# State-space units every 14.4 attention steps in place of 15, and four idle sub-steps in place of eight ahead of the gate products

## The chip, the cores and the metric

One core of one Trainium2 chip runs the whole program. The metric is the device time of one execution in microseconds (us), the median of several executions. The engines are PE (TensorE: matrix products and transposes), DVE (VectorE), ACT (ScalarE), POOL (GpSimd) and SP (SyncE, which here only issues transfers). A transfer is issued by an engine's queue, takes that queue some tenths of a us, and lands later.

## The reference, cut to what matters

One layer of a streaming encoder: 2048 frames of width 1024. A normalised input is projected once; a quarter of the columns, `u`, goes to a state-space mixer, the rest are queries, keys and values of chunked attention. Both results are normalised, joined and sent through `w_out`; then a gated feed-forward network follows.

```python
bu = einsum('bsgh,gph->bsgp', u, b_bar)          # 32 groups of 16 channels, 64 complex states each
_, states = associative_scan(combine, (a, bu))   # along the 2048 frames
y = einsum('bsgp,ghp->bsgh', states, c_mat).real + d_skip * u
y = gelu(y)
y = y * sigmoid(y @ w_glu + b_glu)               # the gate products of the mixing
scores = q k^T / 8 + bias[clip(rel)]             # each 64-frame chunk sees itself and 8 before it
out = softmax(scores) v
```

## The kernel before, in words

Every matrix product is made of three passes of split operands (a high and a low part, tiles named `..h`/`..l` or `hi`/`lo`), so PE has much to do. The program goes through stages one after another: the projection of `u` (0 to 144 us), the attention loop (144 to about 738 us), the mixing (to about 1000 us), the gate and up products of the feed-forward network, and its down product (to the end). Only the attention loop and the first part of the mixing are touched by the change.

**The attention loop** (`att_phase`, L947) has 128 steps: 4 blocks of 512 frames, 8 heads, 4 query tiles. A step s does, in this order: the score products of step s (tiles `sc`, the softmax after them on DVE L846 and ACT L849), on some steps the head's output products (tiles `pj<-pth,v`), the transposes of the probabilities of step s−2 (tiles `pt`, L77; ACT L864 copies them into `pth`, DVE L865 writes the low part `ptl`), and then "filler": pieces of other work, called units. All products on PE are pinned in the order in which the program writes them, so PE never passes a product that waits.

**Units.** A unit is a Python generator with n sub-steps that is to run between attention steps s0 and s1. `Unit.advance` (L667 ff.) is called once in each step and runs as many sub-steps as a proportional rule wants by then (L672). There are units that normalise the input of the next block (`hT_unit`), that project queries and keys (`qk_unit`, tiles `pf`; DVE L775 writes the keys `k` that the scores read) and values (`v_unit`), 8 state-space units, and the mixing's beginning.

**A state-space unit** (`ssm_unit`, L560) handles 4 of the 32 groups in 42 sub-steps:

1. loads on SP (L567): `U` (8 transfers), `Bst`, `Tm` (8), `Vm`; then YL = 8 idle sub-steps;
2. two sub-steps with 4 products each, `pj<-U,Bst`, copied by ACT (L591) into X: called the **X products** here;
3. 21 sub-steps of scan on POOL (L605 to L617), which works only from X;
4. a transfer of the scanned states, `XG<-X`, 4 pieces issued by POOL (L639), then YX = 9 idle sub-steps;
5. two sub-steps with 8 products each, `pj<-U,Tm` and `pj<-XG,Vm`: the **Y products**. ACT copies the result (L649), and SP writes it out in 8 transfers (L652, `y<-X`).

U, Tm, Vm, X and XG are single buffers. The loads of the next unit's U and Tm wait until the Y products of this unit are done, and they stand behind this unit's 8 writes of y on SP. The units follow one another without a break: unit b runs from step 2 + int(SW·b) to step 2 + int(SW·(b+1)).

**The mixing's beginning** (`mix_phase`) is a unit too, of MIX_N sub-steps. At step 119 it loads the gate weights (L997 ff.). From step 122 on it loads the state-space output `yr<-y` (L1030, 4 transfers that need all of y), applies Gelu on ACT (L1034; this loads another activation table first), splits the result into `gh` and `gl` (L165, L166), waits PY idle sub-steps, and then makes the **gate products** `pf<-gh,wgh` etc. in 16 sub-steps, one of them with the norm's sums (`pf<-ones,sq`). Then it loads the second block and waits PZ sub-steps. Its last part runs after the loop.

The lines that the change's numbers enter:

```python
units.append(Unit(ssm_unit(...), SSM_N, 2 + int(SW * b), 2 + int(SW * (b + 1)), light=SL))   # L945
units += [Unit(islice(mix, MIX_N), MIX_N, GSTART, N + LAG, GSTART - OPEN)]                   # L951
want += math.ceil((self.n - 1) * self.room(self.s0, s + 1) / self.room(self.s0, self.s1) - 1e-9)
```

Of the kernel before, what the change touches and what calls it, by code (L numbers as in the profile page):

```python
# [45 lines left out]
LPH = 2  # L46
V0 = 0, 4
DB, XB = 3, 2
SW = 15
CUT = -8, -2, 2, 7, 13, 19, 24  # L50
CUTL = -8, -2, 2, 7, 13, 19, 23
ORDER = "sptf"
# [628 lines left out]
def att_phase(k, ident, S):  # L681
    tc, nc, io = k.tc, k.nc, k.io
    with ExitStack() as cx:
# [260 lines left out]
        for b in range(NG // GB):  # L944
            units.append(Unit(ssm_unit(k, sp, psum, S, b, k.ssm_eng), SSM_N, 2 + int(SW * b), 2 + int(SW * (b + 1)), light=SL))  # L945
        N = len(steps)
# [19 lines left out]
        return mix  # L966


PY, PZ = 8, 1
MIX_N = 17 + PY + PZ  # L970


# [732 lines left out]
```

## Time and profile before

| what | value |
|---|---|
| time, median of 3 executions | 2330.36 us (2327.14 to 2331.63) |
| the profiled execution's own time | 2327.38 us |
| span of the profiled execution (first to last instruction) | 2325.6 us |
| mean granted TensorE clock | 0.971 |
| attention loop, start of step 0 to start of step 127 | 144.1 to 737.8 us |
| transfers issued in the span | 437.00 MB, mean 188 GB/s |

A row of the timeline gives the start and the duration in us, the engine, the line, the operation, what it writes and reads, and in brackets for how long the engine stood idle before it and what ended that. "x8" joins eight like instructions. SPq is SP's queue of transfers. A row of the table by windows gives, for a stretch from A to B, its length, then busy time and (count) of PE, PE's weight loads, DVE, ACT and POOL, then the granted clock of TensorE (1.00 is full), the mean busy share of the transfer engines, and GB/s.

### The profile page before, as it was taken

How to read it: one execution, taken by the hardware profiler on the slowest of the kernel's cores; microseconds unless marked ns; L12 is line 12 of the kernel's file. 1: busy time of each engine (PE TensorE's matmuls, PEld its weight loads, DVE VectorE, ACT ScalarE, POOL GpSimd, SP SyncE). 2: the span in 40 equal slices, each digit the busy share in tenths (PEclk: the TensorE clock that was granted, in tenths of full speed). 3: DMA queues.
4: the chain of work that ended last, by engine and by line, in shares of the span. 5: the costliest groups of instructions: out<-in, count | busy, mean ns of one | idle time of the engine just before them, and what ended most of it. 6: DMA issues, size and time to landing. Idle time of an engine off the chain costs nothing.

```text
span 2325.6 us, 30451 instructions
## 1 busy us (share of the span) xinstructions
PE 2191.2 (94%) x10568; PEld 1839.8 (79%) x10568; DVE 1481.0 (64%) x2251; ACT 1000.5 (43%) x1675; POOL 1130.8 (49%) x1280
## 2 busy tenths in 40 slices
PE   8978899999997899989999998999999989999996
PEld 6667688898986788768888887788888778888886
DVE  7845555656556846666775667766645375578676
ACT  6335555555557542343333335333333343345322
POOL 3406645455660433565555558545555364445442
PEclk9989999999998999999999999999999999999998
DMA  8787766766643535644554556555433287465552
GB/s 296 256 280 259 226 206 199 213 194 193 187 139 114 177 122 170 227 160 149 167 192 162 195 195 239 195 194 167 156 95 110 87 321 251 163 219 181 202 186 73
DMA packets 214066, 437.00 MB, mean 188 GB/s; under 512 B 27096, under 2 KB 57864, under 8 KB 206808
## 3 DMA queue, kind: packets, MB, share of 16 engines
q1 hardware_dynamic: 209048, 420.89, 54.5%
q0 software_dynamic: 4864, 14.17, 1.9%
q8 instruction: 83, 1.36, 0.2%
q14 instruction: 71, 0.58, 0.1%
HBM read 294.98 MB, written 132.15 MB: 184 GB/s over the span
## 4 chain that ended last, share of the span: by engine, by line
PE 50%; DVE 3%; DMA 1%; issue 1%; POOL 1%; ACT 1%; SPq 0%; DVEq 0%; ACTq 0%; POOLq 0%
PE X L74 19%; PE ps L74 16%; PE Y L74 10%; PE W L74 5%; DVE sa L1554 1%; DVE lo L166 1%; DMA hd<-wc 1%; POOL c L166 0%; DMA acc<-x 0%; DVE S L1373 0%; DVE g L1438 0%; DMA hd<-hq 0%; DMA lo<-hc 0%; DVE acc L1571 0%; DVE u L1395 0%
## 5 line engine op out<-in xcount | busy, mean ns | idle before, releaser
L74 PE MATMUL X<-hi,c 128*128 128x512 f32 x1408 | 451.2, 391 | 9.1 <-ACT c L165 5.0
L74 PE MATMUL ps<-hd,hd 128*128 128x512 f32 (+1 forms) x1968 | 433.9, 382 | 7.7 <-POOL hd L166 5.4
L74 PEld LDWEIGHTS ps<-hd,hd 128*128 128x128 f32 x1968 | 359.9, 190 | 80.4 <-POOL hd L166 6.2
L166 POOL TENSOR_TENSOR c<-S,c 128x512 fp32r<-128x512 f32 x176 | 251.4, 1430 | 245.6 <-ACT c L165 244.6
L74 PEld LDWEIGHTS X<-hi,c 128*128 128x128 f32 x1408 | 265.4, 189 | 66.7 <-ACT c L165 5.4
L166 POOL TENSOR_TENSOR hd<-hd 128x1536 fp32r<-128x1536 f32 (+1 forms) x53 | 190.2, 3597 | 207.0 <-ACT hd L165 188.0
L74 PE MATMUL X<-lo,c 128*128 128x512 f32 x704 | 274.9, 390 | 0.0
L166 POOL TENSOR_TENSOR c<-raw,c 128x512 fp32r<-128x512 f32 x132 | 188.1, 1425 | 128.1 <-ACT c L165 100.6
L165 ACT CAST hd<-hd 128x1536 fp32r<-128x1536 f32 (+1 forms) x106 | 147.3, 1392 | 225.4 <-DMA hd<-hq 143.6
L74 PE MATMUL Y<-hi,c 128*128 128x512 f32 x704 | 227.2, 393 | 10.9 <-DVE u L1395 10.9
L1519 DVE TENSOR_TENSOR acc<-acc,ps 128x512 f32<-128x512 f32 x196 | 128.6, 681 | 80.8 <-PE ps L74 80.3
L74 PE MATMUL big<-m,woh 128*128 128x512 f32 x512 | 164.7, 402 | 1.9 <-DVE m L166 1.6
L74 PEld LDWEIGHTS Y<-hi,c 128*128 128x128 f32 x704 | 133.7, 190 | 40.5 <-DVE u L1395 12.6
L74 PE MATMUL pf<-hi,w 128*128 128x512 f32 x416 | 151.7, 417 | 7.3 <-ACT w L165 3.6
L165 ACT CAST c<-S 128x512 fp32r<-128x512 f32 x176 | 109.3, 622 | 111.9 <-PE Y L74 55.9
L605 POOL TENSOR_TENSOR st<-X,a 128x128 f32<-128x128 f32 (+2 forms) x136 | 47.0, 346 | 226.5 <-ACT X L591 164.8
L74 PEld LDWEIGHTS X<-lo,c 128*128 128x128 f32 x704 | 132.8, 189 | 27.4
L846 DVE CUSTOM_DVE_ANT_0 s<-sc,nb 128x640 f32<-128x640 f32 (+4 forms) x128 | 94.4, 738 | 93.3 <-PE sc L74 89.4
L1391 ACT COPY u<-X 128x512 f32<-128x512 f32 x132 | 77.1, 585 | 178.2 <-PE X L74 178.2
L165 ACT CAST c<-raw 128x512 fp32r<-128x512 f32 x132 | 82.1, 622 | 151.0 <-PE Y L74 81.3
L166 DVE TENSOR_TENSOR hd<-hd 128x1536 fp32r<-128x1536 f32 (+1 forms) x53 | 115.3, 2176 | 38.7 <-ACT hd L165 37.6
L74 PE MATMUL Y<-lo,c 128*128 128x512 f32 x352 | 138.2, 393 | 0.0
(463 smaller groups left out, 4693.5 us busy)
## 6 DMA issues: line engine op xcount, KB each, us to landing
w<-wss SPq DMA_DIRECT2D x36, 1024.0 KB, 5.7
hq<-g SPq DMA_DIRECT2D x140, 256.0 KB, 2.0
hd<-hq SPq DMA_DIRECT2D x42, 768.0 KB, 4.5
hd<-wc SPq DMA_DIRECT2D x42, 768.0 KB, 6.1
raw<-in_w_gate SPq DMA_DIRECT2D x44, 512.0 KB, 3.6
raw<-in_w_up SPq DMA_DIRECT2D x44, 512.0 KB, 4.2
wc<-px SPq DMA_DIRECT2D x66, 256.0 KB, 2.9
wss<-w SPq DMA_DIRECT2D x12, 1024.0 KB, 5.8
```

Of the source, the lines that this page charges most:

```text
L74: return self.tc.keep_in_program_order(self.tc.nc.tensor.matmul(*a, **b))
L165: (hi_eng or nc.scalar).copy(hi, raw)
L166: (lo_eng or nc.gpsimd).tensor_tensor(lo, raw, f32(hi), op=ALU.subtract)
L605: eng.tensor_tensor(t[:, :, :, :n], src, ar, op=ALU.mult)
L846: nc.vector.tensor_tensor_reduce(s[:, :nk].rearrange("p (a b) -> p a b", a=nch), ps[:, :nch, :half], hd.nb[:, nk - 1 :: -1].rearrange("p ( ...
L1391: nc.scalar.copy(u[:], ps[:])
L1519: V.tensor_tensor(a, a, ps[:], op=ALU.add)
L1554: (nc.gpsimd if m else nc.vector).tensor_tensor(self.sa[m][:, :n], self.sa[m][:, :n], t[:, :n], op=ALU.add)
```

## The change

```diff
-SW = 15
+SW = 14.4
...
-PY, PZ = 8, 1
+PY, PZ = 4, 1
 MIX_N = 17 + PY + PZ
```

SW sets where the state-space units stand, PY how many idle sub-steps lie between the Gelu of the first block and its gate products. MIX_N falls from 26 to 22, over the same steps 122 to 129. By the order of instructions, the units' products stand at the end of these attention steps:

| unit | 0 | 1 | 2 | 3 | 4 | 5 | 6 | 7 |
|---|---|---|---|---|---|---|---|---|
| X products, before | 4 | 19 | 34 | 49 | 64 | 79 | 94 | 109 |
| X products, changed | 4 | 18 | 32 | 47 | 61 | 76 | 90 | 104 |
| Y products, before | 16 | 31 | 46 | 61 | 76 | 91 | 106 | 121 |
| Y products, changed | 15 | 29 | 44 | 58 | 73 | 87 | 101 | 116 |

From X to Y there were 12 steps in every unit; now there are 11, except in units 2, 4 and 7, which keep 12. From Y to the next X there are 3 steps, before and now. No product is added or left out.

The first place is PE around the start of step 88. `pf_...` are query/key products of the filler of step 87, `sc_...` the scores of step 88, `pt_...` the transposes. Before:

```order
L74 MATMUL pf_6331<-lo_1174_4794,w_6089 128x512
L74 MATMUL pf_6331<-hi_1173_4793,w_6089 128x512
L74 MATMUL sc_6486<-k_1461_6216,q2h_6214 128x320
L74 MATMUL sc_6486<-k_1461_6216,q2l_6215 128x320
...
L77 MATMUL pt_6496<-ident_81,s_6372 128x128 x5
```

With the change:

```order
L74 MATMUL pf_6383<-lo_1178_4810,w_6149 128x512
L74 MATMUL pf_6383<-hi_1177_4809,w_6149 128x512
L74 MATMUL pj_6487<-U_5763,Tm_5774 128x256
L74 MATMUL pj_6487<-XG_2387,Vm_5783 128x256
...
L74 MATMUL pj_6493<-U_5763,Tm_5774 128x256
L74 MATMUL pj_6493<-XG_2387,Vm_5783 128x256
...
L74 MATMUL sc_6507<-k_1481_6276,q2h_6274 128x320
L74 MATMUL sc_6507<-k_1481_6276,q2l_6275 128x320
...
L77 MATMUL pt_6517<-ident_81,s_6406 128x128 x5
```

Unit 5's Y products, which stood at the end of step 91, now stand right in front of the scores of step 88. (The repetitions of the `pj` and `sc` rows are left out.)

The second place is PE at steps 123 and 124, where the gate products begin (`gh`, `gl` are the split Gelu output, `wgh`, `wgl` the split gate weights). Before:

```order
L77 MATMUL pt_8412<-ident_81,s_8265 128x128 x5
L74 MATMUL sc_8420<-k_1848_7995,q2h_7993 128x320
L74 MATMUL sc_8420<-k_1848_7995,q2l_7994 128x320
...
L77 MATMUL pt_8429<-ident_81,s_8306 128x128 x5
L74 MATMUL pf_8437<-gh_1929_8357,wgh_1892_8218 128x512
L74 MATMUL pf_8437<-gl_1930_8358,wgh_1892_8218 128x512
```

With the change:

```order
L77 MATMUL pt_8412<-ident_81,s_8286 128x128 x5
L74 MATMUL pf_8420<-gh_1929_8357,wgh_1895_8239 128x512
L74 MATMUL pf_8420<-gl_1930_8358,wgh_1895_8239 128x512
...
L74 MATMUL sc_8427<-k_1864_8047,q2h_8045 128x320
L74 MATMUL sc_8427<-k_1864_8047,q2l_8046 128x320
...
L77 MATMUL pt_8436<-ident_81,s_8306 128x128 x5
```

The first gate products stand one step earlier: ahead of the scores and transposes of step 124 in place of behind them. The 16 sub-steps of gate products are spread as 2, 3, 3, 3, 3, 2 over steps 124 to 129 before, and as 2, 2, 3, 3, 2, 3, 1 over steps 123 to 129 with the change.

The third place is ACT at the table load ahead of the Gelu (`s_...` is the exponential of the softmax, L849; `pth_...` the copy of the transposes). Before:

```order
L849 ACTIVATE s_8401,sm_8249<-s_8401,mn_8402 128x640
L864 CAST pth_8334<-pt_8412 128x5x128
L849 ACTIVATE s_8425,sm_8249<-s_8425,mn_8426 128x640
L864 CAST pth_8334<-pt_8429 128x5x128
L1034 ACT_TABLE_LOAD
```

With the change:

```order
L849 ACTIVATE s_8401,sm_8270<-s_8401,mn_8402 128x640
L165 CAST wgh_1901_8251<-sg_8253 128x512
L165 CAST wgh_1904_8257<-sg_8259 128x512
L864 CAST pth_8334<-pt_8412 128x5x128
L1034 ACT_TABLE_LOAD
```

The table load now follows the copy of the transposes that belong to step 123, one exponential and one copy earlier, with two weight copies ahead of it.

## The prediction

> **What bounds the kernel now.** The page comes first, with the engines' shares. Then the attention loop alone, in the table by windows, since only the loop and its last steps are touched.
>
> ```profile
> PE 2191.2 (94%) x10568; PEld 1839.8 (79%) x10568; DVE 1481.0 (64%) x2251; ACT 1000.5 (43%) x1675; POOL 1130.8 (49%) x1280
> ```
>
> ```profile
> 144.10:737.80 593.70, 541.21 (x3193) 482.52 (x3194) 330.58 (x638) 324.69 (x672) 294.53 (x708) 0.94 0.66 200
> ```
>
> PE bounds. In the loop it is busy for 541 of 594 us at a clock of 0.94, while DVE, ACT and POOL are busy for about half. A step takes 593.7/127 = 4.67 us. The change takes no product away, so it can only move PE's waits and what they do to the clock. So the second view is the waits of PE inside the loop, the third what the clock did behind them.
>
> ```profile
> PE pt L77 <- DVE ptl L865: 11.6, 9, 2.6
> PE pj L74 <- DMA Tm<-kts: 4.1, 3, 2.4
> ...
> PE pf L74 <- ACT gh L165: 6.8, 1, 6.8
> ```
>
> ```profile
> 225.90:229.30 3.40, 3.35 (x17) 3.02 (x18) 1.08 (x2) 0.64 (x2) 0.00 (x0) 1.00 0.63 212
> 313.30:316.70 3.40, 3.40 (x12) 2.91 (x11) 0.07 (x1) 2.57 (x7) 0.00 (x0) 0.50 0.50 107
> 422.50:425.90 3.40, 3.27 (x11) 2.79 (x12) 3.34 (x7) 2.10 (x4) 0.00 (x0) 0.50 0.96 347
> 552.20:555.60 3.40, 3.40 (x9) 2.68 (x9) 3.34 (x6) 2.13 (x4) 3.35 (x5) 0.50 0.96 351
> 651.20:654.60 3.40, 3.40 (x11) 2.93 (x10) 0.54 (x1) 2.93 (x8) 0.02 (x1) 0.50 0.56 141
> ```
>
> The last four rows lie right behind the four waits of 2.4 to 2.9 us shown below: 3.4 us at half clock, so 1.7 us of work lost. **Such a wait costs its length and 1.7 us more.** The first row, behind a wait of 2.99 us, has full clock: the price is not paid every time.
>
> **The first two units become late.** Shown: the starts of steps 16 and 17, unit 0's Y products, unit 1's X products, step 30, unit 1's Y products and step 32; then POOL's last issue of unit 1's scan, and the landing times of that transfer.
>
> ```profile
> 219.16 0.22 PE L74 MATMUL sc<-k,q2h 128*128 128x128 f32 x1
> 225.95 0.67 PE L74 MATMUL pj<-XG,Vm 128*128 128x256 f32 x2 [2.99 <-DMA XG<-X]
> 228.86 0.47 PE L74 MATMUL sc<-k,q2h 128*128 128x256 f32 x1
> 239.94 1.97 PE L74 MATMUL pj<-U,Bst 128*128 128x256 f32 x8 [0.87 <-DMA Tm<-kts]
> 284.92 0.34 PE L74 MATMUL sc<-k,q2h 128*128 128x384 f32 x1
> 293.51 0.59 PE L74 MATMUL pj<-U,Tm 128*128 128x256 f32 x2
> 296.78 0.50 PE L74 MATMUL sc<-k,q2h 128*128 128x320 f32 x1
> ```
>
> ```profile
> 285.42 1.21 POOL L639 DMA_DIRECT2D XG<-X  x2 [0.30 <-POOL X L617]
> ```
>
> ```profile
> DMA to landing us min/median/max: 7.1/7.6/8.2
> ```
>
> For all eight units together the same view has:
>
> ```profile
> DMA to landing us min/median/max: 2.3/5.0/8.4
> ```
>
> Unit 0's X products stay in step 4, so its XG lands at 225.9 as before, and PE, now at the end of step 15, comes to it at about 219.6: it waits some 6.3 us in place of 2.99. From there a chain that PE doesn't hold up runs on: Y, the writes and loads on SP (PE had to wait 0.87 us for them already), X at 239.9, the scan on POOL, XG issued until 286.6 and landed 7 us later, at about 293.5. Before, PE came to that point at 293.5 too; this is no slack. So unit 1's Y products still end at about 296.8 whatever PE does, but PE has steps 30 and 31 still ahead of it: 293.51 − 284.92 = **+8.6 us**. Behind a wait of about 4 us the products run at half clock (up to +1.7), but a landing in the whole run's median of 5 us in place of 7.6 gives as much back; I leave both out and keep 6 to 10.3 as the bounds.
>
> **Unit 2's load wait goes.** Its X products, and on SP the writes of y and loads of U ahead of them:
>
> ```profile
> 312.51 3.02 PE L74 MATMUL pj<-U,Bst 128*128 128x256 f32 x8 [2.44 <-DMA Tm<-kts]
> ```
>
> ```profile
> 299.32 3.61 SPq L652 DMA_DIRECT2D y<-X  x8
> 304.58 3.41 SPq L567 DMA_DIRECT2D U<-u  x7
> ```
>
> Before, 296.78 to 312.51 = 15.7 us from Y to X, since the writes began 2.5 us after Y and a weight load stood between the two rows. With the change the writes and the loads stand one behind the other: some 0.6 (ACT's copy) + 3.6 + 3.7 (8 loads) + about 2.5 for the landing = 10.4 us by these rows, while PE has steps 30, 31 and 32, 8.6 and a mean step of 4.7, together 13 us. The wait and its half clock vanish: **−4.1** (0 if another load slips between). Unit 3's share of the row Tm<-kts, 4.1 − 2.44 − 0.87 = 0.8, goes likewise; its XG may cost 0.5: **−0.3**.
>
> **Y products fill two waits.**
>
> ```profile
> 418.72 0.41 PE L74 MATMUL sc<-k,q2h 128*128 128x320 f32 x1
> 422.63 1.33 PE L77 MATMUL pt<-ident,s 128*128 128x128 f32 x5 [2.63 <-DVE ptl L865]
> 432.56 0.59 PE L74 MATMUL pj<-U,Tm 128*128 128x256 f32 x2
> ```
>
> ```profile
> 547.85 0.31 PE L74 MATMUL sc<-k,q2h 128*128 128x320 f32 x1
> 551.06 0.42 PE L74 MATMUL sc<-k,q2h 128*128 128x320 f32 x1 [2.76 <-DVE k L775]
> ```
>
> In steps 59 and 88 PE waits for DVE. The Y products, 296.78 − 293.51 = 3.27 us of PE's work, now stand in front of step 59 (unit 3) and of step 88 (unit 5). DVE works on meanwhile, so each wait is filled, with its half clock: −2.63 − 1.7 and −2.76 − 1.7, if the Y products themselves don't wait. For unit 5 that can be checked:
>
> ```profile
> 502.61 0.50 PE L74 MATMUL sc<-k,q2h 128*128 128x320 f32 x1
> 514.45 1.89 PE L74 MATMUL pj<-U,Bst 128*128 128x256 f32 x8
> ```
>
> ```profile
> 557.36 1.21 POOL L639 DMA_DIRECT2D XG<-X  x2 [0.30 <-POOL X L617]
> ```
>
> From X to the last XG issue 558.0 − 514.45 = 43.5, to the landing 46 to 48 (3 to 5 us); PE has from step 77 (502.61) to step 88 (547.85) 45.2: some 0.5 us short. I take **−4.0** for each, with −8 to 0 as the bounds of both. Where step 59's wait is gone, unit 4's load has steps 59 to 61, 432.56 − 418.72 − 4.3 = 9.5 us for 10.4: **+1.3** with what little the other loads may lack, +0.5 more: **+1.8**.
>
> **Unit 7's load wait goes.**
>
> ```profile
> 650.15 2.81 PE L74 MATMUL pj<-U,Bst 128*128 128x256 f32 x8 [2.89 <-DMA U<-u]
> ```
>
> X moves to step 104, away from the block boundary's own loads; three mean steps give 14 us for 10.4: −2.89 − 1.7 = **−4.6** (bounds −4.6 to 0).
>
> **The mixing's beginning.**
>
> ```profile
> 698.28 0.60 PE L74 MATMUL pj<-U,Tm 128*128 128x256 f32 x2
> 701.55 0.50 PE L74 MATMUL sc<-k,q2h 128*128 128x320 f32 x1
> 708.73 0.85 PE L77 MATMUL pt<-ident,s 128*128 128x128 f32 x5 [2.15 <-DVE ptl L865]
> 712.40 1.30 PE L77 MATMUL pt<-ident,s 128*128 128x128 f32 x5 [1.75 <-DVE ptl L865]
> 720.46 0.79 PE L74 MATMUL pf<-gh,wgh 128*128 128x512 f32 x1 [6.76 <-ACT gh L165]
> ```
>
> ```profile
> 714.45 1.28 ACT L1034 ACT_TABLE_LOAD   x1
> 715.74 3.64 ACT L1034 ACTIVATE ys<-yr 128x2048 f32<-128x2048 f32 x1
> ```
>
> The gate products wait 6.76 us for ACT, which does the table load and the Gelu only behind the copy of step 124's transposes. With the change they stand behind step 123's transposes (708.73), and the Gelu one copy earlier, so the **wait remains**: ACT's 1.28 + 3.64 us still lie between those transposes and the first gate product. The transposes are 3.7 us earlier than step 124's; two weight copies (about 0.6 each) and the wait ahead of 712.40 eat part, so the products start 2 to 3 us earlier. But step 124's scores and transposes (3.7 − 1.75 + 1.3, about 2 us at full clock) now follow them. **−0.9**, with −3 to +3 as bounds: this is an order in which I can't see which wait is then last.
>
> Four idle sub-steps fewer are not work; the new ACT copies in front of other steps may uncover waits (the page's waits have nine of `ptl` alone): **+2.0**, bounds 0 and 4.
>
> **The sum** against the profiled execution's 2327.38 us (span 2325.6): 8.6 − 4.1 − 0.3 − 4.0 − 4.0 + 1.8 − 4.6 − 0.9 + 2.0 = −5.5, so 2321.9. That execution was 3.0 under the median of the three, 2330.36; against the median it is **2325 us**.
>
> **A page's rule.** The Trainium skill, "TensorE: Matmul & The Clock Gate", Part 1 (the HAM clock gate), says that the clock halves after at least one idle window of about 3.4 us, and that the windows run free. By that rule waits of 2.4 to 2.9 us would cost no clock, and four removals would bring 4 × 1.7 us less. The rows above disagree on the length (0.50 behind all four) and agree with free-running windows in one point: the same kind of wait at 225.95 left the clock at 1.00.
>
> **The rivals.**
>
> - *The fills don't hold* at steps 59 and 88, since the DVE chains there are themselves set by PE's earlier products: +8, about 2333. For it: waits on `ptl` come nine times, they are not tied to a place. Chance 0.18.
> - *Slower: the scan doesn't fit into 11 steps.* In units 3, 5 and 6 it is as in units 0 and 1: XG lands in 8 us, as unit 1's did. Unit 5 then needs 43.5 + 8 = 51.5 against 45.3, so it waits 6 us in place of 0.5; for units 3 and 6, also 11 steps long, I take 2.5 us each (between nothing and unit 5's 6). With three half clocks of 1.7 this is 5.5 + 5.0 + 5.1 = +15.6, so about 2340. It decides where landings take more than some 5 us. For it: units 0 and 1 are already bound by this chain. Against it: all units' median landing of 5.0 us. Chance 0.20.
> - *The gate wait is hidden*: y is written 5 steps earlier; if the scheduler's order lets ACT do the Gelu before PE needs it, 6.76 + 1.7 go as well: about 2317. Against it: ACT's order puts the table load behind step 123's copy. Chance 0.12.
> - *Short waits cost no clock, and the four half clocks are due to something that stays*: 4 × 1.7 = 6.8 less gain, about 2331. For it: the window at 225.90. Against it: four of five. Chance 0.08.
>
> **How the numbers follow.** Forecast 0.42, around 2325 (2319 to 2330 by its own bounds). 0.2%, 4.7 us, is about what a measurement of this kernel can tell from no change, so faster means under 2325.7 and slower over 2335.0. Two thirds of the forecast (0.28) and the hidden gate wait (0.12) are faster: 0.40. The rest of the forecast (0.14), most of the fills that don't hold (0.13) and most of the fourth rival (0.06) are the same: 0.33. The rest, 0.27, is slower. The range reaches from within the third rival, 2315, to past the second, 2341.
>
> **What would show it.** In the changed profile: a wait of about 6 us on XG near 226 and one of about 4 near 293; no wait of 2.4 on U or Tm at unit 2's X products nor of 2.9 at unit 7's; no wait for `k` in step 88 nor for `ptl` in step 59; full clock there; still 5 to 7 us of wait on `gh`, ending near 718 plus the lag. The forecast is wrong if XG is waited for in units 3, 5 or 6 by more than 1 us, or if waits of 2 to 3 us turn up at new places.

## The result, and the profile after

The changed kernel is **slower**: 2346.60 us (median of 6, 2339.45 to 2349.81) against 2329.64 us (6 runs beside them, 2327.14 to 2331.63), a ratio of 1.007 with a 95% interval of 1.0056 to 1.0084. The forecast was 2325 us, with a range from 2315 to 2341.

Two more waits of PE before the change, from 150 to 720 us (a row has the total in us, how many waits there were, and the longest):

```profile
PE sc L74 <- DVE k L775: 6.6, 3, 2.8
...
PE pf L74 <- ACT hi L729: 3.6, 2, 2.0
```

The waits of PE in the changed kernel, from 150 to 720 us and from 720 to 1000 us:

```profile
PE pj L74 <- DMA XG<-X: 11.6, 2, 6.9
PE pj L74 <- DMA Tm<-kts: 11.2, 3, 5.7
...
PE pt L77 <- DVE ptl L865: 6.6, 7, 1.8
PE pf L74 <- ACT hi L729: 5.4, 2, 3.1
PE sc L74 <- DVE k L775: 4.3, 2, 2.7
...
PE pj L74 <- DMA U<-u: 1.3, 1, 1.3
```

```profile
PE pf L74 <- ACT gh L165: 8.5, 1, 8.5
```

The waits for XG grew from 3.0 to 11.6 us, as forecast. The waits for loads at the X products grew from 7.0 us (4.1 put down to Tm, 2.9 to U) to 12.5 (11.2 and 1.3), which was not; these products read only U and Bst, so the name Tm is not to be taken at its word. The waits for `ptl` and `k` shrank, the one for `hi` grew. The rows with these waits in the timeline of PE, in the order of the units (the XG waits of units 0 and 1, then the X products of units 2, 4, 5 and 7):

```profile
222.44 1.19 PE L74 MATMUL pj<-XG,Vm 128*128 128x256 f32 x2 [4.71 <-DMA XG<-X]
290.39 1.19 PE L74 MATMUL pj<-XG,Vm 128*128 128x256 f32 x2 [6.86 <-DMA XG<-X]
307.07 1.89 PE L74 MATMUL pj<-U,Bst 128*128 128x256 f32 x8
441.49 3.75 PE L74 MATMUL pj<-U,Bst 128*128 128x256 f32 x8 [5.67 <-DMA Tm<-kts]
515.91 3.50 PE L74 MATMUL pj<-U,Bst 128*128 128x256 f32 x8 [4.49 <-DMA Tm<-kts]
645.84 1.89 PE L74 MATMUL pj<-U,Bst 128*128 128x256 f32 x8
```

Units 2 and 7 have no wait any more, as forecast. Units 4 and 5, which had none before, wait 5.67 and 4.49 us, and their eight products take 3.75 and 3.50 us in place of 1.89: the clock is halved there, as the windows show.

```profile
443.70:447.10 3.40, 3.40 (x12) 2.88 (x10) 0.75 (x2) 2.85 (x8) 0.24 (x1) 0.50 0.87 259
515.10:518.50 3.40, 2.58 (x6) 2.17 (x7) 0.00 (x0) 0.45 (x2) 0.00 (x0) 0.57 0.36 68
```

**Where the time went, stretch by stretch.** For some attention steps up to which the same units' products are done in both kernels, the table has the start of the first score product in the two profiled executions, and the lag, after minus before. At step 61, 3.3 us of Y products that stand later before are taken off. The last attention steps can't be compared so, since the changed kernel has made two sub-steps more of gate products by step 127; behind step 112 the table goes on to the mixing's first output product (`big<-m,woh`), ahead of which both have made all of them.

| up to step | before, us | after, us | lag | gained in the stretch | forecast | what lies in it |
|---|---|---|---|---|---|---|
| 15 | 217.03 | 215.02 | −2.0 | −2.0 | 0 | nothing that was changed |
| 52 | 387.68 | 390.27 | +2.6 | +4.6 | +4.2 | units 0 to 3: 8.6 − 4.1 − 0.3 |
| 61 | 430.05 | 433.13 | −0.2 | −2.8 | −4.0 | Y products in front of step 59 |
| 66 | 456.28 | 464.64 | +8.4 | **+8.6** | +1.3 | unit 4's loads |
| 81 | 519.46 | 534.20 | +14.7 | **+6.3** | +0.5 | unit 5's loads |
| 96 | 589.20 | 605.73 | +16.5 | **+1.8** | −4.0 | Y products in front of step 88 |
| 112 | 661.97 | 673.81 | +11.8 | −4.7 | −4.6 | unit 7's loads |
| output product | 763.27 | 777.65 | +14.4 | **+2.6** | −0.9 | the mixing's beginning |
| end (span) | 2325.6 | 2346.9 | +21.3 | +6.9 | 0 | nothing that was changed |

The last row is mostly not the change's: in a run below whose text differs from before only in the queue of some loads inside the loop, the stretch behind the first output product was 4.9 us longer too (lag −10.9 there, −6.0 at the end). The profiled execution of before is 2.3 us under the median of its kernel and that of after 2.2 above, which is why the medians differ by 17.0 us and the spans by 21.3. The allowance of +2.0 for newly uncovered waits has no stretch of its own.

**What holds up units 4 and 5** is on SP's queue. After unit 3's Y products, which end at 425.3 us:

```profile
425.92 0.33 SPq L747 DMA_DIRECT2D k<-ks  x1
427.53 0.46 SPq L771 DMA_DIRECT2D q2h<-q2h  x1
428.62 0.46 SPq L772 DMA_DIRECT2D q2l<-q2l  x1
429.14 5.90 SPq L652 DMA_DIRECT2D y<-X  x8
435.13 0.37 SPq L899 DMA_DIRECT2D ya_s<-ya  x1
435.55 3.72 SPq L567 DMA_DIRECT2D U<-u  x8
```

And after unit 4's Y products, which end at 500.2 us:

```profile
500.85 1.26 SPq L652 DMA_DIRECT2D y<-X  x3
505.84 0.34 SPq L747 DMA_DIRECT2D k<-ks  x1
506.31 0.47 SPq L771 DMA_DIRECT2D q2h<-q2h  x1
507.43 0.47 SPq L772 DMA_DIRECT2D q2l<-q2l  x1
507.95 2.48 SPq L652 DMA_DIRECT2D y<-X  x5
510.47 3.23 SPq L567 DMA_DIRECT2D U<-u  x7
```

The longest wait of this queue from 494 to 518 us that holds up the rows above:

```profile
SPq L747 <- PE sc L74: 3.6, 1, 3.6
```

The writes of y, and behind them the loads of the next U, stand in one queue with the key and query copies of a `qk_unit` (L747, L771, L772). The query copies wait for ACT and DVE, and the key copy waits for score products of PE itself. The last load of U is issued 14.0 and 13.5 us after the Y products, so the products can start 16 us after them; the forecast had 10.4.

### The profile page after: what moved, and what is told of

Read it like the earlier page. It is cut to its first block, busy times and chain, and to the rows that moved or that the text cites. A ratio compares the mean times of both kernels' runs of the same rounds, so it can differ in the third digit from the quotient of the medians.

```text
span 2346.9 us, 30468 instructions
## 1 busy us (share of the span) xinstructions
PE 2195.0 (94%) x10568; PEld 1842.2 (78%) x10568; DVE 1468.7 (63%) x2251; ACT 1000.5 (43%) x1675; POOL 1131.2 (48%) x1280
## 4 chain that ended last, share of the span: by engine, by line
PE 49%; DVE 4%; DMA 1%; issue 1%; POOL 1%; ACT 1%; SPq 0%; DVEq 0%; ACTq 0%; POOLq 0%
PE X L74 19%; PE ps L74 16%; PE Y L74 10%; PE W L74 5%; DVE sa L1554 1%; DMA hd<-hq 1%; DVE lo L166 1%; DMA lo<-hc 0%; POOL c L166 0%; DVE hd L166 0%; DMA acc<-x 0%; DVE S L1373 0%; DVE g L1438 0%; DVE acc L1571 0%; DVE u L1395 0%
```

## The experiments

**SW alone and PY alone.** The first run has the change of SW without that of PY:

```diff
-SW = 15
+SW = 14.4
```

> SW = 14.4 alone, the eight idle sub-steps stay. Theory Q (SP's queue: units 4 and 5 wait 4 to 6 us for loads that stand behind key and query copies on SP, with a half clock behind each): these waits stay, about +14 us in the attention loop, and only the gate part's +3 goes: 2341 to 2344 us against 2329.6 before. Rival G (half of the loss is the gate products that begin before their Gelu): under 2338.

Measured: 2346.83 us, ratio 1.0064 (1.0039 to 1.0088). The waits in front of the X products of units 4 and 5 are 4.65 and 4.42 us, as theory Q has it; rival G is out. The time itself is over the 2341 to 2344 us expected: the gate part's gain does not show in the median. The second run has the other half:

```diff
-PY, PZ = 8, 1
+PY, PZ = 4, 1
```

> PY = 4 alone, SW = 15. All load waits as before. If the earlier place of the gate products costs by itself, because scores and transposes of step 124 no longer cover the Gelu: wait on gh of 8 to 11 us in place of 6.76, 2332 to 2335 us. If the gate's loss in the changed kernel came from the state-space output's load on SP's queue and so from SW: 2330 or less.

Measured: 2334.38 us, ratio 1.0013 (0.9999 to 1.0026), which is not to be told from no change for sure. Its trace shows where it loses: the first gate product with PY = 4, and with SW = 14.4 alone.

```profile
716.14 0.80 PE L74 MATMUL pf<-gh,wgh 128*128 128x512 f32 x1 [10.23 <-ACT gh L165]
```

```profile
733.90 0.80 PE L74 MATMUL pf<-gh,wgh 128*128 128x512 f32 x1 [6.76 <-ACT gh L165]
```

With PY = 4 PE waits 10.23 us, with eight idle sub-steps 6.76. From step 123 to the mixing's first output product the execution with PY = 4 loses 4.0 us to the one before (lag −4.1 to −0.1), 3.5 of them in this wait. With SW = 14.4 the wait is 8.49 us in place of 6.76, and the same stretch takes 59.4 us with four idle sub-steps and 54.9 with eight. So the earlier place costs 4 to 4.5 us in the traces with either SW; but in the two kernels with SW = 14.4 nothing of it can be seen in the medians, 2346.6 and 2346.8.

**U's loads on another queue.** In the changed kernel and in the one before, POOL issues the eight loads of U for units 1 to 7; its queue holds only XG and the scan:

```diff
-    def load(out, in_):
-        ins = nc.sync.dma_start(out, in_)
+    def load(out, in_, q=nc.sync):
+        ins = q.dma_start(out, in_)
...
-        load(U[j * CH : (j + 1) * CH], S["u"][...])
+        load(U[j * CH : (j + 1) * CH], S["u"][...], eng if b else nc.sync)
```

> The changed kernel with the 8 loads of U (units 1 to 7) issued by POOL, whose queue holds nothing else then, in place of SP. Theory Q: the waits of 5.67 and 4.49 us in front of the X products of units 4 and 5 go, with two half clocks, about -13 us: 2332 to 2335. Rival R (the load waits are transfer traffic, not the queue's order, or the lateness only moves to the next wait): 2342 or more.

Measured: 2343.51 us, ratio 1.0056 (1.0035 to 1.0077): by its time, rival R. The trace tells it apart. The loads of U behind unit 4's Y products (which end at 492.9 us), the X products of units 4 and 5, then unit 5's XG product:

```profile
492.72 4.05 POOL L567 DMA_DIRECT2D U<-u  x8 [12.50 <-PE pj L74]
```

```profile
435.52 1.89 PE L74 MATMUL pj<-U,Bst 128*128 128x256 f32 x8
503.92 1.89 PE L74 MATMUL pj<-U,Bst 128*128 128x256 f32 x8
553.51 1.19 PE L74 MATMUL pj<-XG,Vm 128*128 128x256 f32 x2 [3.61 <-issue]
```

Both load waits are gone, with full clock. At step 84 PE is 1.5 us behind the kernel before in place of 14.4, where at step 61 the two kernels with SW = 14.4 were within 0.2 us of each other: the queue was worth **12.9 us** there. Then unit 5's Y products wait 3.61 us, at half clock behind it. The profile names no releaser; the last piece of XG was issued at 550.0 us, and its pieces take 3.1 to 5.2 us to land. By step 96 the lag is 9.0 in place of 16.5, so 5.4 of the 12.9 us are given back here, and 3.3 are left at the end of the span. So theory Q holds for the cause, and part of its price was given back in the next link of the unit's chain: X to XG in eleven steps, the mechanism of the prediction's second rival. In the changed kernel the load wait hid this: ACT's copies of unit 5's X began 2.1 us behind the start of the products there, and 4.6 here.

> The kernel before with the same move of the 8 U loads to POOL. Theory Q: its load waits of 2.44 us (unit 2) and 2.89 us (unit 7) go with two half clocks, and the small ones of units 1 and 3: -6 to -10 us, 2320 to 2324. Rival R: 2328 or more, and the waits turn up elsewhere.

Measured: 2321.60 us against 2331.40, ratio 0.9965 (0.995 to 0.9981), **faster than both kernels**, as theory Q has it. The X products of units 2 and 7, which waited 2.44 and 2.89 us before:

```profile
308.20 1.89 PE L74 MATMUL pj<-U,Bst 128*128 128x256 f32 x8
640.31 1.89 PE L74 MATMUL pj<-U,Bst 128*128 128x256 f32 x8
```

With twelve steps from X to Y nothing is given back: the lag at step 112 is −11.1 us. The loads of U, issued at 295.8 to 299.3 us, right behind unit 1's Y products, land in 2.5 to 3.5 us.

**The writes of y on ACT.** On top of U's loads on POOL, with both parts of the change:

```diff
-                nc.sync.dma_start(S["y"][...], Y[j * CH : (j + 1) * CH])
+                nc.scalar.dma_start(S["y"][...], Y[j * CH : (j + 1) * CH])
```

> The changed kernel with U's loads on POOL as in the run before, and the 8 writes of y issued by ACT right behind its copy, so nothing of the units stands behind key and query copies on SP. In the run with U alone on POOL, unit 5's X copies came 4.6 us behind their products, and PE then waited 3.61 us for XG in step 87. If the X buffer, still being written out as y, held them back (theory B): that wait goes with its half clock, -5 us against that run. If unit 5's 11 steps are too short for the scan anyway, or ACT's 8 issues delay the softmax (rival): no gain, or slower.

Measured: 2408.76 us, ratio 1.0334 (1.0314 to 1.0353). ACT's queue and, behind it, PE after unit 0's Y products:

```profile
231.77 7.28 ACTq L652 DMA_DIRECT2D y<-X  x8
239.09 0.40 ACT L849 ACTIVATE s<-s,mn 128x128 f32<-128x128 f32 x1 [6.84 <-DMA y<-X]
```

```profile
243.18 1.09 PE L77 MATMUL pt<-ident,s 128*128 128x128 f32 x4 [9.15 <-DVE ptl L865]
```

The eight issues keep ACT from the softmax for 7 us, and at six places PE waits 5.9 to 13.7 us on the transposes. That is the rival, at more than I would have given it; theory B isn't tested by this run. It can be decided from the run before it, where the last write of y was issued at 502.6 us and the writes land 2.0 to 5.1 us after their issue, so by 507.7 at the latest:

```profile
507.71 0.83 ACT L849 ACTIVATE s<-s,mn 128x640 f32<-128x640 f32 x1
508.44 0.19 ACT L849 ACTIVATION_READ_ACCUMULATOR s<-s,mn 128x1 f32 x1
508.54 3.01 ACT L591 COPY X<-pj 64x256 f32<-64x256 f32 x8
```

The copies start only at 508.54, and ACT has no idle time in front of them: it comes from key copies and softmax work that stand ahead in its order. So theory B is wrong: ACT's own order, not the buffer, sets the start of unit 5's scan, 4.6 us behind its products.

**Eight idle sub-steps with U on POOL, and eleven.**

```diff
-PY, PZ = 4, 1
+PY, PZ = 8, 1
```

> The changed kernel with U's loads on POOL, but eight idle sub-steps as before. If four idle sub-steps cost by themselves as with SW = 15 (there +5 us between step 123 and the mixing): 4 to 5 us less than with four. If the earlier y of SW = 14.4 has taken that cost away: the same within 2 us, with the wait on gh 6.8 in place of 8.3 us but a later place.

Measured: 2336.81 us, ratio 1.0028 (1.0015 to 1.0042), against 1.0056 with four: 6.5 us less, the first case. From step 123 to the mixing's first output product 3.6 us are gained in place of 2.5 lost, a difference of 6.1 us. (The profiled execution is 5.3 us earlier at step 123 already; in it PE waits 2.11 us in place of 8.59 for unit 1's XG, which the number of idle sub-steps does not reach.)

```diff
-PY, PZ = 8, 1
+PY, PZ = 11, 1
```

> SW = 15 with U's loads on POOL and eleven idle sub-steps, so that the gate products begin one step later than before, behind the transposes of step 125. If the cost of the gate's place is the attention work that is left to cover table load and Gelu: the wait on gh falls from 6.9 to about 3 us, -2 to -4 us against the kernel with eight, 2318 or so. Rival: the gate products that are pushed behind the loop's last steps cost as much: the same 2321.

Measured, with SW = 15 and U on POOL: 2329.38 us, ratio 0.9998 (0.9985 to 1.001), so 8 us are lost against eight sub-steps; my expectation and the rival both missed. The first gate product and the norm's sums:

```profile
711.10 0.79 PE L74 MATMUL pf<-gh,wgh 128*128 128x512 f32 x1 [6.76 <-ACT gh L165]
718.68 1.80 PE L74 MATMUL pf<-ones,sq 128*128 128x1 f32 x8 [3.12 <-DVE sq L1014]
```

The wait on `gh` is the same 6.76 us one step later: the Gelu moved with the gate products, since in ACT's order its table load now stands behind one more copy of the transposes. At none of the three places did moving the products alone cover the wait.

**One step more for unit 5.** The units' bounds written out, so that unit 5 has 12 steps from X to Y:

```diff
-SW = 14.4
+US = 2, 16, 30, 45, 59, 74, 89, 103, 118
...
-2 + int(SW * b), 2 + int(SW * (b + 1)), light=SL
+US[b], US[b + 1], light=SL
```

> The run with SW = 14.4, U's loads on POOL and eight idle sub-steps, but unit 5 has one step more (its Y products stand in step 88 in place of 87, and units 6 and 7 one step later, with unit 7 still two steps earlier than with SW = 15). Theory F (eleven steps do not hold unit 5's scan): the wait of 3.6 to 3.9 us for XG falls under 1.5 us, its half clock goes, and the lag that PE gains from step 84 to step 96 falls from +7.5 to about +3; 2332 against 2337. But step 88's wait for k, which the Y products no longer precede, should come back (2.1 to 2.8 us) if PE is early enough. Rival: the wait for XG is a matter of the copies of X on ACT, which come some 4.6 us behind the products, and keeps 2 to 3 us.

Measured: 2337.43 us, ratio 1.003 (1.0021 to 1.0039), the same as the run with eight idle sub-steps, where 2332 was expected. Step 88 in this run, and unit 5's XG product at its end:

```profile
553.57 0.42 PE L74 MATMUL sc<-k,q2h 128*128 128x320 f32 x1 [3.19 <-DVE k L775]
```

```profile
557.03 0.59 PE L74 MATMUL pj<-XG,Vm 128*128 128x256 f32 x2
```

The wait for XG is gone, with full clock, so theory F is right on the step; the lag from step 84 to step 96 grows by 3.1 us in place of 7.5, where most of the difference lies between steps 90 and 96 (the wait on `hi` told of below goes too). But the wait for `k` in step 88 is back, 3.19 us, and the time is no better. In this execution PE waited 6.5 us longer for unit 1's XG (8.59 us); how much of the 4 us shows in the median can't be told from one profile.

## Why the prediction was wrong, point by point

The sum came to −5.5 us, and the profiled execution to +21.3. Of these 26.8 us, 13.1 come from the loads of units 4 and 5, 5.8 from the stretch around step 88, 3.5 from the mixing's beginning, and 6.9 from the part behind it, which is mostly not the change's; everything else together takes 2.5 off.

- **PE bounds, and only waits and the clock can move: right.** PE's busy time is 2191.2 and 2195.0 us.
- **Units 0 to 3: right.** PE comes 4 to 7 us too early to the XG of units 0 and 1 (4.71 and 6.86 us for 6.3 and about 4), unit 2's load wait goes; +4.6 us for +4.2.
- **Unit 7: right**, −4.7 for −4.6.
- **The failed step is the one on the loads of the other units**: "unit 4's load has steps 59 to 61, 432.56 − 418.72 − 4.3 = 9.5 us for 10.4", with +1.8 for all the loads of units 4 to 6. The steps that PE has were right; the 10.4 us of the load chain were not. That sum held the issues and the landing, but not what stands ahead in SP's queue. Unit 2's 15.7 us of before, shown there, had been put down to a weight load in between and taken as the exception; with the change units 4 and 5 come to stand beside the key and query copies and need 16 us. Measured: +8.6 and +6.3 in place of +1.8. The sign stood in the profile before the change, where the same copies are ahead of unit 7's loads, the other load wait that was to go:

```profile
638.39 0.32 SPq L747 DMA_DIRECT2D k<-ks  x1
639.04 0.47 SPq L771 DMA_DIRECT2D q2h<-q2h  x1
639.99 0.46 SPq L772 DMA_DIRECT2D q2l<-q2l  x1
640.50 3.99 SPq L652 DMA_DIRECT2D y<-X  x8
```

Moving the loads to POOL's queue took 12.9 us of it away at step 84, which shows the queue as the cause.
- **Unit 5's scan** was short by the prediction's own rows: 46 to 48 us to the landing against 45.2 are 1 to 3 us, not 0.5. In the changed kernel no such wait is seen; with U on POOL's queue it is 3.61 us.
- **The Y products in front of steps 59 and 88: half right.** Step 59 gave 2.8 for 4.0, since a wait of 0.93 for `ptl` comes back in step 60. In step 88 the wait for `k` is indeed gone, and up to step 90 the lag falls by 3.6 us (with the Y products taken off). But a wait on the next block's input comes two steps later:

```profile
580.05 0.50 PE L74 MATMUL pf<-hi,w 128*128 128x512 f32 x1 [2.30 <-ACT hi L729]
```

with half clock behind it:

```profile
580.25:583.65 3.40, 3.18 (x8) 2.32 (x8) 1.16 (x2) 0.59 (x1) 0.00 (x0) 0.53 0.16 33
```

From step 90 to step 96, 5.4 us are lost, so the whole stretch lost 1.8 in place of gaining 4.0. I had asked whether the Y products wait, not which wait is next behind them. The new wait comes with the units' place: all four traces with unit 5's Y products in step 87 and y written from SP's queue have it, at 2.29 or 2.30 us, and lose 5.3 to 5.4 us from step 90 to 96, also where PE is ahead of the kernel before (U on POOL, eight idle sub-steps):

```profile
567.65 0.80 PE L74 MATMUL pf<-hi,w 128*128 128x512 f32 x1 [2.30 <-ACT hi L729]
```

With unit 5's Y and unit 6's X products one step later it is gone, and 2.2 us are lost. By which link the place sets ACT's and DVE's work is not shown.
- **The mixing's beginning**: the wait remains, as the prediction says, but the cost of the earlier place was mis-sized: +2.6 in place of −0.9, with 8.49 us of wait for 6.76. The run with PY alone loses 4.0 us by it, and eight sub-steps with U on POOL take 6.1 us away.

```profile
717.69 1.24 SPq L1030 DMA_DIRECT2D yr<-y  x2
```

```profile
724.22 1.28 ACT L1034 ACT_TABLE_LOAD   x1 [1.52 <-issue]
725.51 3.64 ACT L1034 ACTIVATE ys<-yr 128x2048 f32<-128x2048 f32 x1
```

Here too SP's queue takes part: the last write of y was issued at 701.8 us, but the last two loads of `yr` are issued at 717.69 to 718.93, behind two weight loads that wait for a buffer. Whether they or the table load end that wait was not tried.

The Trainium skill, "Trainium Kernel Development and Optimization", Key Constraints, says that issuing transfers from several engines only saves the time of issuing. Here eight issues take 3.7 us on SP, so 7.4 for units 4 and 5, and moving them saved 12.9 us there: the trace disagrees where an earlier entry of the queue waits for another engine. The same skill, "TensorE: Matmul & The Clock Gate", Part 1 (the HAM clock gate), has the clock halve behind an idle window of about 3.4 us: the wait of 2.30 us at 580.05 was followed by a clock of 0.53 (580.25 to 583.65), the one of 3.19 us above by full clock (1.00 from 553.57 to 556.97). The trace agrees with windows that run free, not with the length as a bound.

## What to carry to other kernels

Before a piece of work is moved in a hand-made order, look up what stands ahead of its transfers in the queue that issues them, at the new place, and for what each entry waits; the sum of issues and landing is only the lower bound of a load. Where such a chain is serial (load, product, scan, transfer, product), price each link against its slack at the new spacing, since a wait that is removed only uncovers the next one. A transfer that must be prompt belongs on a queue whose other entries don't wait: here that alone made the kernel of before 0.35% faster. Such a queue must not be that of an engine whose next instruction is wanted soon: with U on POOL's queue the changed kernel was 0.6% slower than before, and with the writes of y on ACT as well 3.3%.

## What the runs showed of the hardware that was not expected

Eight issues of 16x4x256 writes kept ACT from its next instruction for 6.84 us (the queue's row shows 7.28), while eight loads of the same shape took POOL about 4.1 us (each 0.512) and SP 3.7. The part of the program behind the mixing's first output product, which no edit touched, took 2 to 8 us longer in the profiles of all other runs than in the one of before; no run here shows why.
